# Hybrid encoder layer on one core: four modulation vectors in a lane of their own, last-norm rows on VectorE, causal mask on VectorE or GpSimd

## The chip, the cores and the metric

One core of one Trainium2 chip runs the whole layer in one launch. The metric is the device time of that launch in microseconds (us); a lower time is better. TensorE does the matrix products and the transposes, VectorE (DVE) and GpSimd (POOL) the elementwise work, ScalarE (ACT) the activations and some copies, and SyncE (SP) issues every DMA, in order.

## The reference, cut to what matters

```python
mod = (silu(c) @ w_ada + b_ada).reshape(bsz, 3, 3, 1024)      # nine vectors of 1024
f1 = _swiglu(_modulate(x, mod[:, 0, 0], mod[:, 0, 1]), ffn1_w_up, ffn1_w_down)
x = _post_norm(x, 0.5 * f1, mod[:, 0, 2], ln1_g, ln1_b)
tm = _token_mixer(_modulate(x, mod[:, 1, 0], mod[:, 1, 1]), w_in, ...)   # mLSTM heads | S5 groups
x = _post_norm(x, tm, mod[:, 1, 2], ln2_g, ln2_b)
f2 = _swiglu(_modulate(x, mod[:, 2, 0], mod[:, 2, 1]), ffn2_w_up, ffn2_w_down)
x = _post_norm(x, 0.5 * f2, mod[:, 2, 2], ln3_g, ln3_b)
```

There are 1024 tokens of 1024 channels, the hidden width of a feed-forward part is 2816, everything is float32. `_post_norm` is a layer norm of `alpha*x + (1+gate)*f`. The S5 part of the mixer needs tables (powers of a complex diagonal and products with its input and output matrices) that depend on parameters alone.

## The kernel before

**Products.** Each float32 operand is split into a high and a low part of a reduced type (`split`: a copy, then a subtraction), and a product is three matmuls 128x128 by 128x512 (`mm3`). All recorded times carry line 79, the place where the kernel's recording layer emits an instruction, so instructions are told apart by engine, shape and tile: `s` is any of 99 on-chip buffers of 256 KB, `b` a bank of PSUM.

**Feed-forward.** The first three column blocks of 128 of the hidden layer are plain products (`up_jobs`); the others come in pairs and are done by seven products in place of eight (`pair_jobs`, named by f = 3 and up; a pair job is 84 big matmuls). Their results go to DRAM as `Td`. The down projection does seven passes over the blocks (`product_jobs`, p = 5, 6, 3, 1, 7, 2, 4), which load `Td` and `in_w_down` (`w_down`) again. At the end of passes 1 and 7, sixteen and twelve VectorE instructions combine the four banks (`out`).

**Order.** TensorE's jobs run in a fixed list. All other work is written as generators in named lanes. A planner (`Clock`, `Kern.issue`) keeps a running clock of costs for every engine and, between TensorE's steps, takes from the lanes what is ready, earlier lanes first; each lane has a margin and a number of buffers that it must leave free (`LANES`). `nc.any` gives an addition or a product to VectorE or GpSimd, whichever the planner has free first. The program that results is fixed: every engine, and SP with it, runs its list in order.

**The lane `bg`** starts once the first modulated input is done. It computes the modulations 2 to 8 of the nine (`ada`; 0 and 1 are done in the start-up): for each, 16 loads of 256 KB of `in_w_ada`, 64 matmuls of 32 columns (`32x128` in the order, `128*32 128x128` in the trace, where each is recorded twice), and column sums with `one`. Then follow `affine` and `cols` for the later norms, and then `s5_gen`, which makes the S5 tables and stores them as `Wd`, `Vd`, `Md` and, last, sixteen `Ed`. The first norm waits for `("affine", 1)`, the S5 mixer for `("tables",)`.

**Last norm.** The last four hidden blocks are applied row tile by row tile (`end_jobs`): 8 transposes and 24 big matmuls for each of 8 tiles of 128 tokens. `end_ln` finishes a tile: copies and additions into buffers, statistics (`est`, `emv`), a reciprocal square root of some ten one-column instructions on `er` (`rsqrt`), then ScalarE scales and shifts, GpSimd (the first five tiles) or `any` multiplies by the gain and adds the bias. The last tile is done by two VectorE instructions per half instead.

**Mask.** In `mlstm`, sixteen additions on GpSimd (`P.tensor_tensor`) add the causal mask to blocks 128x512 before ScalarE's exponential.

Of the kernel before, what the change touches and what calls it, by code (L numbers as in the profile page):

```python
# [10 lines left out]
AF = mybir.ActivationFunctionType  # L11
OP = mybir.AluOpType
# [227 lines left out]
class Stream:  # L240
# [120 lines left out]
    def ensure(self, c):  # L361
        while self.ns <= min(c + AHEAD_SPLIT, len(self.chunks) - 1):
# [8 lines left out]
LANES = {"startl": (3.5, 20), "startx": (3.5, 2), "start": (3.5, 2), "startw": (3.5, 2), "startm": (4.5, 8),  # L371
# [3 lines left out]
WINDOW = 24  # L375
U, Q = ("u0", "u1", "u2", "u3"), ("q2", "q3", "q0", "q1")
IN_ORDER = ([(x, 0) for x in U + ("g", "q2")] + [(x, 1) for x in U + ("g", "q2")]
            + [(x, h) for x in Q[1:] + ("v", "o") for h in range(2)])
# [1 line left out]
S5_LATE = False  # L380
NACT = 4
SPARE = 8
END_POOL = 5
START_N = 1
START_A = 4
START_G = (0, 4), (4, 8)
# [9 lines left out]
class Kern:  # L396
# [483 lines left out]
    def pair_jobs(self, w_up, f, sub):  # L880
        nc, st = self.nc, self.st
        V = nc.vector
        cs = st.add_pair(*(w_up[f, u, :, 4 * y:4 * y + 4].rearrange("p k m -> p (k m)") for u in range(2) for y in range(2)))
        x = {}

        mix, block = {1: 0, 2: 1, 4: 2, 6: 3}, {0: (0, 0), 5: (4, 0), 3: (4, 1)}
        home, opens, closes = "adadaba", (0, 1, 5), (3, 5, 6)
        bank = {}  # L890

        def right(p, k):
            if p in mix:
                return self.T[mix[p]][k]
            k0, h = block[p]
            return self.Mh[k0 + k][h], self.Ml[k0 + k][h]

        def drop(p, k):
            if p in mix:
                self.T[mix[p]][k] = None  # L900
            else:
                k0, h = block[p]
                self.Mh[k0 + k][h] = self.Ml[k0 + k][h] = None

        def keep(n, b):
            x[n] = self.S()
            nc.scalar.activation(x[n], b, AF.Copy)

        def plus(n, b):
            V.tensor_tensor(x[n], x[n], b, op=OP.add)  # L910

        def out(p, b):
            if p in (0, 1, 2):
                keep(p, b)
            elif p == 3:
                plus(2, b)
                nc.scalar.activation(x[2], x[2], AF.Silu)
            elif p == 4:
                plus(1, b)
                nc.any.tensor_tensor(x[1], x[1], x.pop(2), op=OP.mult)  # L920
                self.hidden(sub, f, 1, x.pop(1))
            elif p == 5:
                plus(0, b)
                nc.scalar.activation(x[0], x[0], AF.Silu)
            else:
                g = x.pop(0)
                V.tensor_tensor(g, g, b, op=OP.mult)
                self.hidden(sub, f, 0, g)

        def job(p):  # L930
            def run():
                if f == NPLAIN[sub] and p == 0:
                    for k in range(4):
                        self.Mh[k][1] = self.Ml[k][1] = None
                if p in opens:
                    bank[home[p]] = self.bank()
                b = bank[home[p]]
                wh, wl = st.get(cs[p])
                for k in range(4):
                    c = slice(k * 128, (k + 1) * 128)  # L940
                    rh, rl = right(p, k)
                    mm3(nc, b, wh[:, c], wl[:, c], rh, rl, p in opens and k == 0, k == 3, p not in opens)
                    if f == NF - 1:
                        del rh, rl
                        drop(p, k)
                    if k == 1:
                        yield
                out(p, b)
                if p in closes:
                    self.free(b)  # L950
                yield
            return run

        for p in range(7):
            self.jobs.append(Job(cs[p], job(p), (("t", sub),) if f == NPLAIN[sub] and p == 0 else ()))
# [237 lines left out]
    def end_ln(self, t, banks):  # L1193
        nc = self.nc
        V = nc.vector
        st = self.small("est", [128, 2, 6], 4)
        mv = self.small("emv", [128, 2], 4)
        r = self.small("er", [128, 4], 4)
        xs = [self.S() for _ in range(2)]
        for y in range(2):  # L1200
            x = banks[y]
            if len(banks) == 4:
                nc.copy(xs[y], banks[2 + y])
                V.tensor_tensor(xs[y], xs[y], banks[y], op=OP.add)
                x = xs[y]
            V.bn_stats(st[:, y, :], x)
        V.bn_aggr(mv, st)
        V.tensor_scalar(r[:, 0:1], mv[:, 1:2], LN_EPS_S, None, op0=OP.add)
        last = len(banks) == 2
        for y in range(2 if last else 0):  # L1210
            V.scalar_tensor_tensor(xs[y], banks[y], mv[:, 0:1], self.gain[y], op0=OP.subtract, op1=OP.mult)
        self.rsqrt(r[:, 1:2], r[:, 0:1], r[:, 2:3])
        if not last:
            V.scalar_tensor_tensor(r[:, 3:4], mv[:, 0:1], -1.0, r[:, 1:2], op0=OP.mult, op1=OP.mult)
        for y in range(2):
            x = xs[y]
            if last:
                V.scalar_tensor_tensor(x, x, r[:, 1:2], self.gain[2 + y], op0=OP.mult, op1=OP.add)
            else:
                nc.scalar.activation(x, x, AF.Identity, scale=r[:, 1:2], bias=r[:, 3:4])  # L1220
                e = nc.gpsimd if t < END_POOL else nc.any
                e.tensor_tensor(x, x, self.gain[y], op=OP.mult)
                e.tensor_tensor(x, x, self.gain[2 + y], op=OP.add)
            nc.sync.dma_start(self.O["out"][t * 128:(t + 1) * 128, y * 512:y * 512 + 512], x)
        self.free(*banks)
        yield
# [918 lines left out]
    def mlstm(self):  # L2145
# [26 lines left out]
        for j, cs in enumerate(pairs):  # L2172
# [6 lines left out]
            for x, c in enumerate(cs):  # L2179
                hc, ts = self.tok(c)  # L2180
                mrs = ms[x]
                for d in range(2):
                    P.tensor_tensor(mrs[d], mrs[d], mk[:, d].unsqueeze(1).to_broadcast([128, 4, 128]), op=OP.add)
                sb = [self.bank(), self.bank()]
                for a in range(2):
                    nc.tensor.transpose(sb[0][:, (a + 2) * 128:(a + 3) * 128], qk[2 + a, hc][:, ts], self.ident)
                self.KT[c] = kt[:, x]
                nc.scalar.activation(self.KT[c], sb[0][:, 256:].rearrange("p (h x) -> p h x", h=4), AF.Copy)
                for a in range(2):
                    for p in range(2):  # L2190
                        l = slice(p * 64, p * 64 + 64)
                        nc.tensor.matmul(sb[p][:, a * 128:(a + 1) * 128], qk[2 + a, hc][l, ts], qk[a, hc][l, ts],
                                         start=True, stop=True)
                for d in range(2):
                    for h in range(4):
                        nc.scalar.activation(mrs[d][:, h, :], mrs[d][:, h, :], AF.Exp, scale=-1.0,
                                             bias=gc[:, c, 0, d, h:h + 1])
                    for p in range(2):
                        V.tensor_tensor(mrs[d][:, p::2, :], mrs[d][:, p::2, :],
                                        sb[p][:, :256].rearrange("p (h t) -> p h t", h=2), op=OP.mult)  # L2200
                    self.PT[d, c] = mrs[d]
                self.mark(("vis", c))
                del mrs
                ms[x] = None
                yield
# [129 lines left out]
    def run(self):  # L2335
# [6 lines left out]
        def background():  # L2342
            yield from self.wait(("m", 0, 1))
            yield from self.ada([2])
            self.cols(0, True)
            self.mark(("cols", 0))
            yield from self.ada(range(3, 9))
            self.cpad = None
            self.affine(1, "ln1_g", "ln1_b")
            self.cols(1, False)  # L2350
            self.affine(2, *(("ln2_g", "ln2_b") if mixer else ("ln1_g", "ln1_b")))
            self.cols(2, True)
            for x in (("affine", 1), ("affine", 2), ("cols", 1), ("cols", 2)):
                self.mark(x)
            if mixer:
                yield from self.s5_gen()
                self.mark(("tables",))

        self.later("bg", background())
        self.ffn(0, I["w_up1"], I["w_down1"], "ln1_g", "ln1_b", nxt, I["x"], skip=3,  # L2360
                 drains=((("m", 0, 0), ("pieces",)), (("m", 0, 1),)))
        if mixer:
# [87 lines left out]
```

## Time and profile before

| | us |
|---|---|
| median of 3 runs (lowest to highest) | 1933.21 (1928.89 to 1936.46) |
| the profiled execution, own time | 1935.63 |
| its span | 1933.8 |
| TensorE busy in the span | 1849.7 (96%), 10544 matmul records |
| VectorE busy | 1587.7 (82%) |
| ScalarE busy | 653.4 (34%) |
| GpSimd busy | 200.5 (10%) |

A busy time is the union of an engine's instructions; for TensorE their ends are modelled, so that a stretch with 100% can still hold fewer matmuls than fit. The chain that ended last is TensorE for 81% of the span, VectorE for 10% and DMA for 5%. The mean granted clock of TensorE is 0.981 of full speed.

### The profile page before, as it was taken

To read this page: it belongs to the slowest core of one execution; us is meant where nothing else is said; L and a number is where in the kernel's file an instruction comes from. 1 tells how busy PE (TensorE), PEld (TensorE's weight loads), DVE (VectorE), ACT (ScalarE), POOL (GpSimd) and SP (SyncE) were. 2 spreads that over 40 slices of the span, in tenths; PEclk is the share of its full clock that TensorE was granted. 3 is DMA by queue.
4 is the path that set the end of the run, shared out by engine and by line. 5 is a ranking of instruction groups with operands and counts; after the bars stand their busy time and mean duration, and the time that the engine had idled before them with its cause. 6 is when DMAs were issued, how large, how long until landed. Compare 5 with 4: busy or idle time off the path is not lost.

```text
span 1933.8 us, 29721 instructions
## 1 busy us (share of the span) xinstructions
PE 1849.7 (96%) x10544; PEld 1458.2 (75%) x10544; DVE 1587.7 (82%) x3296; ACT 653.4 (34%) x1204; POOL 200.5 (10%) x210
## 2 busy tenths in 40 slices
PE   6999999999999899999999998999999999999996
PEld 4667888777788677777787777678888888887775
DVE  7937889989899999868887796998677767597887
ACT  4512333333332325624444422542222222233412
POOL 0000000000000001100014401301111211000014
PEclk9999999999999989998999999999999999999998
DMA  9985233444493735572624544223232323574512
GB/s 324 317 300 192 82 113 115 158 132 141 149 341 117 259 132 190 161 259 100 207 72 150 177 149 157 77 102 111 88 122 96 105 82 109 181 255 143 183 44 76
DMA packets 188148, 303.13 MB, mean 157 GB/s; under 512 B 27792, under 2 KB 47440, under 8 KB 188000
## 3 DMA queue, kind: packets, MB, share of 16 engines
q1 hardware_dynamic: 188000, 301.24, 46.1%
q8 instruction: 83, 1.36, 0.3%
q14 instruction: 65, 0.53, 0.1%
HBM read 224.55 MB, written 76.61 MB: 156 GB/s over the span
## 4 chain that ended last, share of the span: by engine, by line
PE 81%; DVE 10%; DMA 5%; issue 2%; ACT 1%; SPq 1%; DVEq 0%; POOL 0%; ACTq 0%
PE b L79 81%; DVE s L79 8%; DMA s<-in_w_ada 2%; ACT s L79 1%; DMA s<-Vd 1%; SPq L79 1%; DMA s<-in_x 1%; DMA s<-in_w_down 1%; DVE er L79 0%; DMA s<-in_w_first 0%; DMA s<-in_w_f 0%; DMA s<-Td 0%; DVE mr L79 0%; DMA s<-in_w_out 0%; DVE st L79 0%
## 5 line engine op out<-in xcount | busy, mean ns | idle before, releaser
L79 PE MATMUL b<-s 128*128 128x512 f32 (+5 forms) x9208 | 1819.9, 372 | 50.8 <-DVE s L79 36.0
L79 PEld LDWEIGHTS b<-s 128*128 128x128 f32 (+3 forms) x9208 | 1417.0, 177 | 424.0 <-DVE s L79 51.8
L79 DVE TENSOR_TENSOR s<-s 128x512 fp32r<-128x512 f32 (+5 forms) x1767 | 997.6, 613 | 61.8 <-ACT s L79 28.3
L79 ACT ACTIVATE s<-s 128x512 fp32r<-128x512 f32 (+3 forms) x683 | 400.1, 624 | 591.6 <-DVE s L79 386.7
L79 DVE TENSOR_TENSOR s<-s,b 128x512 f32<-128x512 f32 (+1 forms) x340 | 214.8, 653 | 184.6 <-PE b L79 172.6
L79 POOL TENSOR_TENSOR s<-s 128x512 f32<-128x512 f32 (+1 forms) x117 | 169.4, 1464 | 1190.1 <-ACT s L79 502.1
L79 ACT ACTIVATE s<-b 128x512 f32<-128x512 f32 (+3 forms) x219 | 119.5, 553 | 458.8 <-PE b L79 425.0
L79 DVE CAST s<-s 128x512 fp32r<-128x512 f32 (+1 forms) x249 | 129.6, 524 | 7.7 <-DMA s<-in_x 2.7
L79 DVE SCALAR_TENSOR_TENSOR s<-b,gcol,s 128x512 f32<-128x512 f32 x56 | 39.5, 746 | 23.9 <-PE b L79 23.9
L79 ACT ACTIVATE s<-b,vec 128x128 f32<-128x128 f32 (+4 forms) x61 | 25.8, 485 | 88.6 <-PE b L79 82.4
L79 POOL MEMSET s<- 128x4 f32 (+6 forms) x62 | 6.9, 137 | 391.8 <-PE b L79 259.5
L79 PE MATMUL b<-ident,s 128*128 128x128 f32 (+1 forms) x208 | 30.9, 279 | 3.7 <-DVE s L79 3.7
L79 PEld LDWEIGHTS b<-ident,s 128*128 128x128 f32 (+1 forms) x208 | 25.2, 151 | 11.0 <-ACT s L79 4.3
L79 ACT ACTIVATE s<-s,vec 128x512 f32<-128x512 f32 x30 | 22.4, 782 | 19.4 <-DVE s L79 19.4
L79 DVE SCALAR_TENSOR_TENSOR s<-s 128x320 f32<-128x320 f32 (+3 forms) x43 | 22.8, 533 | 6.2 <-ACT s L79 6.0
L79 DVE TENSOR_TENSOR_SCAN s<-s 128x512 f32<-128x512 f32 (+2 forms) x22 | 24.1, 1121 | 4.4 <-POOL s L79 4.3
L79 DVE SCALAR_TENSOR_TENSOR s<-s,vec 128x512 f32<-128x512 f32 (+1 forms) x36 | 25.8, 737 | 0.1
L79 ACT ACTIVATE s<-s,Bp,Gp 128x512 f32<-128x512 f32 x23 | 17.7, 805 | 20.3 <-DVE s L79 20.3
L79 PEld LDWEIGHTS b<-one,s 128*32 128x32 f32 x576 | 8.5, 113 | 15.6 <-DVE s L79 12.2
L79 PE MATMUL b<-one,s 128*32 128x1 f32 x576 | 9.3, 174 | 11.4 <-DVE s L79 11.4
L79 DVE SCALAR_TENSOR_TENSOR s<-s,dec,b 128x129 f32<-128x129 f32 x24 | 8.1, 343 | 14.5 <-PE b L79 14.2
L79 ACT ACTIVATE s<-s,gcols 128x128 f32<-128x128 f32 x64 | 19.6, 394 | 0.2
(102 smaller groups left out, 328.4 us busy)
## 6 DMA issues: line engine op xcount, KB each, us to landing
s<-in_w_up SPq DMA_DIRECT2D x170, 256.0 KB
s<-in_w_ada SPq DMA_DIRECT2D x144, 256.0 KB
Td<-s SPq DMA_DIRECT2D x140, 256.0 KB
s<-Td SPq DMA_DIRECT2D x140, 256.0 KB
s<-in_w_down SPq DMA_DIRECT2D x124, 256.0 KB
Xd<-s SPq DMA_DIRECT2D x48, 256.0 KB
s<-Xd SPq DMA_DIRECT2D x48, 256.0 KB
s<-in_x SPq DMA_DIRECT2D x32, 256.0 KB
```

The costliest lines, as they stand in the source:

```text
L79: self.eng, self.alts, self.emit = eng, (), lambda: getattr(real, name)(*args, **kw)
```

## The change

Lane `bg` now does modulations 2, 3 and 4, then `affine(1)`, then the S5 tables at once. Modulations 5 to 8 with `cols(1)`, `affine(2)` and `cols(2)` move to a new lane `bg2`, last in priority, which waits for the flag `("pair", 0, 5)` that the first job of pair f = 5 of the first feed-forward sets. `end_ln` does every tile as the last one was done: two `scalar_tensor_tensor` on VectorE per half, none of it on ScalarE or GpSimd. The mask addition is given to `any`.

```diff
-         "lv": (3.0, 10), ..., "conv": (2.5, 6), "bg": (3.5, 6)}
+         "lv": (3.0, 10), ..., "conv": (2.5, 6), "bg": (3.5, 6), "bg2": (3.5, 8)}
+LATE = ("pair", 0, 5)
...
+                if p == 0:
+                    self.flags.add(("pair", sub, f))
...
-        last = len(banks) == 2
-        for y in range(2 if last else 0):
-            V.scalar_tensor_tensor(xs[y], banks[y], mv[:, 0:1], self.gain[y], op0=OP.subtract, op1=OP.mult)
+        for y in range(2):
+            x = xs[y] if len(banks) == 4 else banks[y]
+            V.scalar_tensor_tensor(xs[y], x, mv[:, 0:1], self.gain[y], op0=OP.subtract, op1=OP.mult)
         self.rsqrt(r[:, 1:2], r[:, 0:1], r[:, 2:3])
-        if not last:
-            V.scalar_tensor_tensor(r[:, 3:4], mv[:, 0:1], -1.0, r[:, 1:2], op0=OP.mult, op1=OP.mult)
         for y in range(2):
             x = xs[y]
-            if last:
-                V.scalar_tensor_tensor(x, x, r[:, 1:2], self.gain[2 + y], op0=OP.mult, op1=OP.add)
-            else:
-                nc.scalar.activation(x, x, AF.Identity, scale=r[:, 1:2], bias=r[:, 3:4])
-                e = nc.gpsimd if t < END_POOL else nc.any
-                e.tensor_tensor(x, x, self.gain[y], op=OP.mult)
-                e.tensor_tensor(x, x, self.gain[2 + y], op=OP.add)
+            V.scalar_tensor_tensor(x, x, r[:, 1:2], self.gain[2 + y], op0=OP.mult, op1=OP.add)
...
-                    P.tensor_tensor(mrs[d], mrs[d], mk[:, d]..., op=OP.add)
+                    nc.any.tensor_tensor(mrs[d], mrs[d], mk[:, d]..., op=OP.add)
...
-            yield from self.ada(range(3, 9))
+            yield from self.ada([3, 4])
+            self.affine(1, "ln1_g", "ln1_b")
+            self.mark(("affine", 1))
+            if mixer:
+                yield from self.s5_gen()
+                self.mark(("tables",))
+
+        def rest():
+            yield from self.wait(LATE)
+            yield from self.ada(range(5, 9))
             self.cpad = None
-            self.affine(1, "ln1_g", "ln1_b")
             self.cols(1, False)
             ...
-            if mixer:
-                yield from self.s5_gen()
-                self.mark(("tables",))
         self.later("bg", background())
+        self.later("bg2", rest())
```

The planner orders everything anew. Three places follow, as the built programs have them.

SP's list of DMAs in the first feed-forward's down projection, kernel before, from the middle of pass p = 1 (`Ed` are stores of S5 tables, `in_x` loads of the residual, of which each of the passes 3, 1, 7 and 2 has one group of four):

```order
L79 DMA s<-in_x 128x512 x4
L79 DMA Ed<-s 128x512
L79 DMA s<-Td_91 128x512
L79 DMA s<-Td_92 128x512
L79 DMA Ed<-s 128x512
L79 DMA s<-in_w_down 128x512
L79 DMA s<-Td_93 128x512
L79 DMA Ed<-s 128x512 x2
```

The same place in the changed program:

```order
L79 DMA s<-in_x 128x512 x4
L79 DMA s<-Td_91 128x512
L79 DMA s<-Td_92 128x512
L79 DMA s<-in_w_down 128x512
L79 DMA s<-Td_93 128x512
L79 DMA s<-in_w_down 128x512
L79 DMA s<-Td_94 128x512
L79 DMA s<-in_w_down 128x512
```

Before, all sixteen `Ed` stores stand behind the first group of `in_x` loads, that of pass 3; now fourteen stand ahead of it and two right behind it, and none behind the second group.

TensorE's list of the changed program where modulation 4 ends and modulation 5 begins (`32x128` are modulations, `32x1` their column sums, `128x512` big matmuls):

```order
L79 MATMUL b<-s 128x512 x6
L79 MATMUL b<-one,s 32x1 x16
L79 MATMUL b<-s 128x512 x282
L79 MATMUL b<-s 32x128 x12
L79 MATMUL b<-s 128x512 x6
L79 MATMUL b<-s 32x128 x12
```

Before, groups of modulations and groups of six big matmuls alternate without such a gap until the last modulation is done; now 282 big matmuls stand between the third and the fourth of the seven. Counted over TensorE's first 1950 big matmuls, a group of others follows a group of big ones 88 times before and 94 times now.

VectorE's list in the last norm, one of the middle tiles, kernel before (`emv` are a tile's mean and variance, `er` the columns of its reciprocal root):

```order
L79 TENSOR_TENSOR s<-s,b 128x512 x2
L79 BN_STATS est<-s 128x6
L79 SCALAR_TENSOR_TENSOR er<-er 128x1
L79 BN_STATS est<-s 128x6
L79 SCALAR_TENSOR_TENSOR er<-er 128x1
L79 BN_AGGR emv<-est 128x2
L79 TENSOR_SCALAR er<-emv 128x1
L79 TENSOR_TENSOR er<-er 128x1
```

And in the changed program:

```order
L79 TENSOR_TENSOR s<-s,b 128x512 x2
L79 BN_STATS est<-s 128x6
L79 SCALAR_TENSOR_TENSOR er<-er 128x1
L79 BN_STATS est<-s 128x6
L79 TENSOR_TENSOR er<-er 128x1
L79 BN_AGGR emv<-est 128x2
L79 SCALAR_TENSOR_TENSOR er<-er 128x1
L79 TENSOR_SCALAR er<-emv 128x1
L79 SCALAR_TENSOR_TENSOR s<-s,emv 128x512 x2
```

A tile's two centring instructions (`s<-s,emv`) now stand behind its variance, and two scaling ones (`s<-s,er`) follow its reciprocal root. Twenty-eight such instructions of 128x512, in all, are new on VectorE there; twenty products and additions leave GpSimd and eight leave VectorE, and fourteen activations leave ScalarE. Of the sixteen mask additions nine go to VectorE, the first four among them, and seven stay on GpSimd.

## Rows read from the trace of the kernel before

**Rows 1.** Stretches: length, busy us (instructions) by engine, granted clock, DMA share, GB/s

```profile
52.00:162.00 110.00, 108.59 (x1638) 76.30 (x1628) 68.62 (x135) 38.59 (x75) 7.64 (x4) 1.00 0.89 310
162.00:654.00 492.00, 492.00 (x2367) 392.38 (x2357) 449.11 (x1037) 162.83 (x289) 6.39 (x19) 1.00 0.45 152
654.00:760.00 106.00, 93.04 (x439) 73.55 (x438) 104.23 (x175) 32.83 (x56) 7.20 (x5) 0.92 0.57 198
...
1775.00:1816.00 41.00, 36.20 (x149) 28.58 (x148) 37.68 (x61) 17.25 (x30) 0.00 (x0) 0.96 0.51 164
...
1300.00:1350.00 50.00, 50.00 (x218) 40.46 (x217) 43.04 (x70) 11.25 (x19) 6.86 (x5) 1.00 0.38 132
...
550.00:650.00 100.00, 100.00 (x433) 81.01 (x432) 94.88 (x172) 32.90 (x58) 3.46 (x2) 1.00 0.62 218
```

**Rows 2.** TensorE's groups by form in 654 to 760: count, busy, mean ns, idle

```profile
L79 PE MATMUL b<-s 128*128 128x512 f32 x369 | 92.3, 411 | 12.2 <-DVE s L79 12.2
```

**Rows 3.** The chain that ended last, 650 to 762: start, us, what

```profile
666.39 4.98 DMA s<-in_w_down
671.38 4.58 DMA s<-Td
...
704.46 4.00 DMA s<-in_w_down
708.53 5.26 DMA s<-in_x
```

**Rows 4.** SP's queue in time, 640 to 760: start, us, what was issued

```profile
684.23 0.32 SPq L79 DMA_DIRECT2D s<-Td  x1
698.90 0.32 SPq L79 DMA_DIRECT2D Ed<-s  x1
...
708.53 2.28 SPq L79 DMA_DIRECT2D s<-in_x  x4
723.53 3.34 SPq L79 DMA_DIRECT2D Ed<-s  x2
```

**Rows 5.** TensorE's groups by form in 52 to 162, the stretch of modulations

```profile
L79 PE MATMUL b<-s 128*128 128x512 f32 x279 | 76.0, 410 | 0.0
L79 PE MATMUL b<-s 128*32 128x128 f32 x896 | 34.7, 278 | 1.4 <-DMA s<-in_w_ada 1.2
```

**Rows 6.** Groups by form in 1860 to 1934, the last norm

```profile
L79 POOL TENSOR_TENSOR s<-s 128x512 f32<-128x512 f32 x20 | 25.2, 1289 | 63.6 <-ACT s L79 63.5
L79 DVE SCALAR_TENSOR_TENSOR er<-er 128x1 f32<-128x1 f32 x48 | 12.1, 261 | 0.5
...
L79 DVE TENSOR_TENSOR er<-er 128x1 f32<-128x1 f32 x24 | 8.5, 353 | 0.3
```

**Rows 7.** VectorE in time, last norm: start, us for all, what, count

```profile
1871.86 1.28 DVE L79 TENSOR_TENSOR s<-s,b 128x512 f32<-128x512 f32 x2
1873.05 1.28 DVE L79 BATCH_NORM_STATS2 est<-s 128x6 f32<-128x512 f32 x2
...
1876.74 0.16 DVE L79 SCALAR_TENSOR_TENSOR er<-emv,er 128x1 f32<-128x1 f32 x1
...
1907.16 0.15 DVE L79 TENSOR_TENSOR er<-er 128x1 f32<-128x1 f32 x1
...
1917.88 1.18 DVE L79 TENSOR_TENSOR er<-er 128x1 f32<-128x1 f32 x1
...
1929.47 1.41 DVE L79 SCALAR_TENSOR_TENSOR s<-s,er 128x512 f32<-128x512 f32 x2
```

**Rows 8.** GpSimd and TensorE in time, last norm

```profile
1911.56 8.83 POOL L79 TENSOR_TENSOR s<-s 128x512 f32<-128x512 f32 x7 [2.41 <-ACT s L79]
...
1912.00 5.79 PE L79 MATMUL b<-s 128*128 128x512 f32 x24
```

**Rows 9.** Groups by form in 1028 to 1145, the mLSTM stretch

```profile
L79 POOL TENSOR_TENSOR s<-s 128x512 f32<-128x512 f32 x18 | 24.5, 1394 | 2.4 <-DMA s<-Wr 2.4
...
L79 DVE TENSOR_TENSOR s<-s 128x512 f32<-128x512 f32 x6 | 4.5, 771 | 0.0
```

More of the change, by code (lines that the diff above doesn't have):

```diff
@@ L382 @@
 SPARE = 8
-END_POOL = 5
 START_N = 1
@@ L2182, in mlstm @@
                 for d in range(2):
-                    P.tensor_tensor(mrs[d], mrs[d], mk[:, d].unsqueeze(1).to_broadcast([128, 4, 128]), op=OP.add)
+                    nc.any.tensor_tensor(mrs[d], mrs[d], mk[:, d].unsqueeze(1).to_broadcast([128, 4, 128]), op=OP.add)
                 sb = [self.bank(), self.bank()]
@@ L2352, in background @@
             self.cols(2, True)
-            for x in (("affine", 1), ("affine", 2), ("cols", 1), ("cols", 2)):
+            for x in (("affine", 2), ("cols", 1), ("cols", 2)):
                 self.mark(x)
-            if mixer:
-                yield from self.s5_gen()
-                self.mark(("tables",))
         self.later("bg", background())
+        self.later("bg2", rest())
         self.ffn(0, I["w_up1"], I["w_down1"], "ln1_g", "ln1_b", nxt, I["x"], skip=3,
```

2 rows, old and new, of the table LANES are left out of this document.

## The prediction

> **What bounds the kernel now.** I read the view of stretches first: TensorE's busy time and VectorE's beside it, stage by stage [rows 1]. Where TensorE runs at its own pace it does 218 big matmuls in 50 us, 0.230 us each (1300 to 1350). From 162 to 654, the pair products, it is busy all of 492 us, with VectorE at 449.1 of 492 (91%); from 550 to 650 VectorE stands at 94.9 of 100 and TensorE still loses nothing. From 654 to 760, the end of the first down projection, VectorE is full, 104.2 of 106 us, and TensorE's clock falls to 0.92: it did 369 big matmuls there [rows 2], 369 x 0.230 = 84.9 us, and some 70 small ones, 2.4 us by the price below, so 106 - 84.9 - 2.4 = 18.7 us are lost. The second feed-forward's down projection has the same passes without the S5 tables; it loses, from 1775 to 1816, 41 - 149 x 0.230 = 6.7 us.
>
> The chain of waits says how the loss comes about [rows 3]: twice TensorE waits for weights that were asked for late, at 666 and at 704. SP's queue in time gives the reason [rows 4]: after a load at 684.2 it issues nothing for 14 us, until an `Ed` store, whose data VectorE has not yet made, goes out at 698.9; the loads queued behind it follow at once. It stands still again until 723.5. So in this stretch the tables cost twice, as VectorE work and as stores that hold back an in-order queue.
>
> At the other end, TensorE's last big matmuls end at 1912.0 + 5.8 = 1917.8 [rows 8] and VectorE's last instruction at 1929.5 + 1.4 = 1930.9 [rows 7]; the span ends 2.9 us later. The last norm is VectorE's.
>
> **Tables out of the down projection.** By SP's list fourteen of the sixteen `Ed` stores now stand ahead of the first residual loads, none behind the second. Each stands for three VectorE instructions of 128x512 at 1.28 / 2 = 0.64 us [rows 7]; nine were stored after 653.8, three of them in [rows 4], so about 9 x 3 x 0.64 = 17 us of 104 leave, and VectorE is at 87 of 106, no longer the bound. What is late next is the combining work at the ends of passes 1 and 7, which the second feed-forward shows at 6.7 us. Gain 18.7 - 6.7 = 12.0; I take **-11**, since the next norm's first work starts in the same stretch. Bounds: 0, if other work fills the room, to -18.7.
>
> **Where the tables go.** 16 x 3 x 0.64 = 31 us of VectorE work enter the pair products, and four modulations give that stage 26 us more of TensorE (below): (449 + 31) / (492 + 26) = 93%, under the 95% at which TensorE lost nothing [rows 1]. That hides it; I take **+1**. If the cover is gone, it is the slow rival.
>
> **Four modulations moved.** From 52 to 162 the seven modulations cost TensorE 110 - 279 x 0.230 = 45.8 us beside the big matmuls [rows 5] (the other 1638 - 279 = 1359 records [rows 1] then cost 0.034 us each, waits for loads in it). Four of seven are 26.2 us, paid now, by TensorE's list, among 168 big matmuls of the pairs: the same work elsewhere. Two things can differ. By the lists groups of other matmuls follow big ones 94 times for 88, some 30 of these in the old stretch; a group costs at most 45.8 / 30 = 1.5 us, its work included; for the switch alone I take a fifth of it, 0.33, and 6 x 0.33 = **+2** (bounds 0 to +9). And the loads: 64 of `in_w_ada`, 8 of `w_up` and 8 stores stand between them on SP, 80 x 0.262 MB = 21 MB in 168 x 0.230 + 26.2 = 64.8 us, 324 GB/s, where the old stretch moved 310 GB/s with its 16 DMA engines 89% busy [rows 1]. At 310 they need 67.7 us, and weights queued behind them come up to 3 us late; against that, the waits for `in_w_ada` in the old stretch (1.2 us seen) shrink: **+0.7** (bounds -2 to +5). TensorE's share between, 282 big matmuls without a modulation, waits for nothing that is new.
>
> **Last norm on VectorE.** Before a tile: two additions 1.28, two statistics 1.28, a run of small instructions from 1874.3 to 1876.9, 2.6 us [rows 7]. Added: four `scalar_tensor_tensor` at 1.41 / 2 = 0.70, 2.8 us. Alone that is 8.0 a tile; but the order puts the small ones of one tile between the large ones of the next, and half of their 2.6 hidden gives 6.7. I take 7.0, against TensorE's 6.4 (24 big matmuls, 5.8, and the transposes). From 1871.9: seven tiles to 1920.9, the eighth 1.28 + 2.57 + 2.8 to 1927.5, the store 2.9: 1930.4 for 1933.8, **-3.4**. The 8 products that leave VectorE and the wait for ScalarE and GpSimd at the end are what pays for it. Bounds: 6.7 gives -5.5.
>
> The upper bound comes from the small instructions. While GpSimd worked, from 1911.6 on [rows 8], one of one column took 1.18 us; with GpSimd idle, at 1907.2, 0.15 [rows 7]. The change leaves GpSimd idle there. At the means with GpSimd at work, 0.261 and 0.353 [rows 6], they make 3.1 us a tile, which is the second rival's price.
>
> The Trainium skill ("SBUF — State Buffer", section "Who interferes with whom") has it that a VectorE instruction with two inputs in SBUF and a GpSimd instruction that reads SBUF exclude each other for the whole instruction. The trace agrees: 1.18 us is about one GpSimd product (8.83 / 7 = 1.26). By that rule the small ones cost 0.15 once GpSimd is out; without it, the second rival.
>
> **Mask.** Nine of sixteen additions move from GpSimd, at 1.39, to VectorE, at 0.77 [rows 9]: 7 us more on VectorE across four pairs of chunks, while the first blocks come sooner. Queued behind them on VectorE are the products with the scores. **-0.5** (bounds -3 to +4).
>
> **Sum.** -11 + 1 + 2 + 0.7 - 3.4 - 0.5 = -11.2. Against the profiled execution's own 1935.6: 1924.4. That execution lies 2.4 above the median of its runs, so for the median **1922.0**, own range 1914 to 1930.
>
> **Rivals.** First, the down projection keeps its loss: passes' ends and the next norm fill VectorE again, and the term is 0, not -11: 1933. For it speaks that much of VectorE's work there is not the tables'; against it that the second feed-forward runs the same passes at 6.7.
>
> Second, VectorE becomes the bound of the last norm at the means of [rows 6]: 1.28 + 1.28 + 3.1 + 2.99 = 8.7 a tile; 7 x 8.7 + 8 from 1871.9 is 1940.8, with the store 1943.7, +10 for -3.4: 1935. Against it: those means hold waits for GpSimd. The Trainium skill ("Perfetto Trace Analysis", section "Optimizing Scalar/DVE Operations") advises to offload from a saturated VectorE, even to GpSimd, and in the same breath warns that the two share a port. Its first half is this rival; no run shown here decides it.
>
> Third, slower: VectorE runs full in the pair products, where the tables and the moved modulations meet, for the 160 us or so from pair 5 on. The price is that of the one stretch in which it was full, 18.7 / 106 = 0.18 us lost per us, 28 us: 1922 - 1 + 28 = 1949. It decides from between 95% (nothing lost) and 98% (104.2 of 106). For it: 31 us in a stage at 91%; against it the 26 us that the stage grows by. That the change does not do what it says, tables no earlier, is out by SP's list.
>
> **How the numbers follow.** About 0.5%, 9.7 us, is what a measurement of this kernel can tell from no change. Forecast 0.63 (0.53 under 1923.5, 0.10 above); first rival 0.12, no change; second 0.14, 0.13 of it no change; third 0.11, slower. Faster 0.53, same 0.35, slower 0.12. The range 1911 to 1940 takes in the forecast's bounds and both middle rivals and leaves out the third.
>
> **What would show it.** Right: in the down projection's stretch VectorE under 95%, no SP pause ahead of an `Ed`, the granted clock above 0.92; TensorE busy all through the pairs; in the last norm no one-column instruction of 1 us, the end 12 to 14 us after the last big matmul. Wrong: TensorE's waits on `DVE s` between pairs, VectorE without a pause there, or a last norm in which tiles follow each other by 8 us and more.

## The result, and the profile after

The changed kernel took a median of 1910.7 us in 6 runs (1908.4 to 1919.2), the kernel before beside it 1933.7; the ratio is 0.9888, with a 95% interval from 0.9862 to 0.9914. A second set of runs of the same kernel, further below, gave 1908.6 us and 0.9867 (0.9841 to 0.9893). So it is faster, by 22 to 26 us. The direction is the one forecast. The time lies at the very edge of the range 1911 to 1940 (the second set a little under it) and outside the forecast's own 1914 to 1930, and the gain is about twice the 11.2 us that were summed. The profiled execution took 1908.43 us, its span 1906.6, with a mean granted clock of 0.987 where before had 0.981.

The page of the changed kernel, busy time by engine and the shares of the chain that ended last:

```profile
PE 1841.5 (97%) x10544; PEld 1453.0 (76%) x10544; DVE 1588.2 (83%) x3306; ACT 646.8 (34%) x1201; POOL 166.5 (9%) x182
...
PE 84%; DVE 10%; DMA 3%; issue 2%; ACT 1%; SPq 0%; POOL 0%; DVEq 0%; POOLq 0%
```

TensorE has 84% of the chain, for 81 before, and DMA 3 for 5; VectorE's busy time is the same 1588 us in a span 27 us shorter. The stretches of the changed kernel that answer to [rows 1]: length, busy us and instructions of PE, PEld, DVE, ACT, POOL, then granted clock, DMA share, GB/s:

```profile
52.00:162.00 110.00, 109.45 (x967) 83.03 (x966) 98.79 (x265) 42.06 (x75) 3.24 (x1) 1.00 0.54 189
162.00:654.00 492.00, 491.62 (x3005) 385.34 (x3004) 439.17 (x944) 162.85 (x293) 7.91 (x21) 1.00 0.55 191
...
654.00:760.00 106.00, 99.38 (x469) 78.76 (x468) 94.85 (x160) 40.08 (x69) 7.23 (x4) 0.95 0.45 146
```

From 52 to 162 TensorE has 967 records in place of 1638: four of the seven modulations have left. In the pairs it is busy all the time still, with VectorE at 439 of 492. From 654 to 760 VectorE is at 94.9 of 106 (89%) and TensorE at 99.4, for 104.2 and 93.0 before.

Every trace has the same 6944 records of matmuls of 512 columns, so that the n-th of them is the same work in all kernels. The table gives the time between such marks, in us: up to the 186th (start-up; from the next one on TensorE's lists differ), to the 2316th (modulations, pairs, first three passes), to the 2844th (the passes 1, 7, 2, 4), to the S5 mixer's first matmul (rest of the first norm and of the in-projection), to the run of 144 big matmuls that ends the mixer, to the second norm's first matmul with `meanw` (the mLSTM and the output projection), to the first of the last 24, and to the end of the span. "Before's lists" are the profiles of this kernel and of the runs below that keep its lists in that stretch, "new lists" those with the change's; with the count of profiles.

| stretch | before | changed | before's lists | new lists |
|---|---|---|---|---|
| to 186 | 97.2 | 96.7 | the same lists in both: 96.4 to 100.4 | |
| to 2316 | 543.7 | 542.8 | 542.3 to 543.9 (5), mean 543.5 | 542.8 to 543.2 (7), mean 542.9 |
| to 2844 | 142.8 | 136.3 | 142.7 to 142.9 (4), mean 142.8 | 134.7 to 136.3 (7), mean 135.4 |
| to S5 | 44.5 | 40.5 | 44.3 to 44.8 (5), mean 44.6 | 39.9 to 40.5 (7), mean 40.1 |
| S5 mixer | 124.5 | 117.1 | 117.4 to 124.5 (5) | 116.3 to 122.5 (8) |
| to second norm | 255.9 | 252.0 | 255.9 to 260.7 (8), mean 257.6 | 251.4 to 252.0 (3), mean 251.8 |
| to the last 24 | 703.5 | 704.4 | 703.5 to 704.2 (6) | 703.6 to 706.4 (7), mean 704.3 |
| to the end | 21.8 | 17.0 | 21.8 to 21.9 (6) | 17.0 to 17.1 (6), 18.2 (1) |

### The profile page after: what moved, and what is told of

Read it like the earlier page. It is cut to its first block, busy times and chain, and to the rows that moved or that the text cites. A ratio compares the mean times of both kernels' runs of the same rounds, so it can differ in the third digit from the quotient of the medians.

```text
span 1906.6 us, 29677 instructions
## 1 busy us (share of the span) xinstructions
PE 1841.5 (97%) x10544; PEld 1453.0 (76%) x10544; DVE 1588.2 (83%) x3306; ACT 646.8 (34%) x1201; POOL 166.5 (9%) x182
## 4 chain that ended last, share of the span: by engine, by line
PE 84%; DVE 10%; DMA 3%; issue 2%; ACT 1%; SPq 0%; POOL 0%; DVEq 0%; POOLq 0%
PE b L79 84%; DVE s L79 9%; DMA s<-in_w_ada 1%; DMA s<-Vd 1%; ACT s L79 1%; DMA s<-in_x 0%; SPq L79 0%; POOL s L79 0%; DMA s<-in_w_first 0%; DVE lnv L79 0%; DMA s<-Td 0%; DMA Ud<-s 0%; DMA s<-Ud 0%; DVE gv L79 0%; DVE er L79 0%
## 5 line engine op out<-in xcount | busy, mean ns | idle before, releaser
L79 PE MATMUL b<-s 128*128 128x512 f32 (+6 forms) x9208 | 1813.4, 371 | 39.0 <-DVE s L79 26.9
L79 PEld LDWEIGHTS b<-s 128*128 128x128 f32 (+4 forms) x9208 | 1412.2, 176 | 409.5 <-DVE s L79 45.5
L79 ACT ACTIVATE s<-s 128x512 fp32r<-128x512 f32 (+4 forms) x680 | 399.0, 625 | 557.7 <-DVE s L79 409.2
L79 ACT ACTIVATE s<-b 128x512 f32<-128x512 f32 (+2 forms) x220 | 119.7, 553 | 461.2 <-PE b L79 410.6
L79 POOL TENSOR_TENSOR s<-s 128x512 f32<-128x512 f32 (+2 forms) x88 | 132.8, 1520 | 1158.4 <-ACT s L79 566.8
L79 DVE CAST s<-s 128x512 fp32r<-128x512 f32 x252 | 128.1, 511 | 8.5 <-DMA s<-in_x 3.2
L79 DVE SCALAR_TENSOR_TENSOR s<-s,vec 128x512 f32<-128x512 f32 (+1 forms) x36 | 25.7, 734 | 0.1
L79 PE MATMUL b<-one,s 128*32 128x1 f32 x576 | 9.4, 174 | 11.9 <-DVE s L79 11.9
L79 DVE SCALAR_TENSOR_TENSOR s<-s,gcol 128x512 f32<-128x512 f32 x24 | 18.3, 764 | 0.6
```

The lines of the kernel that those rows point to most:

```text
L79: self.eng, self.alts, self.emit = eng, (), lambda: getattr(real, name)(*args, **kw)
```

## The experiments

**The three parts alone, and two of them.** The lists of the engines show that the parts don't touch each other: the lanes' end in the S5 mixer, the mask begins in the mLSTM, the norm's edit changes only the last norm. So each was built alone on the kernel before, and lanes and norm together. The lanes (`background` and `rest` as in the change, norm and mask as before):

> The lanes alone: tables ahead of the four modulations, norm and mask as before. Theory 1 (all of the gain up to the last norm comes from the lanes, that in the first norm, the in-projection and the S5 mixer too, since TensorE's, VectorE's and SP's lists differ from those of before only up to there): 1933 - 9.5 (down projection) - 10.7 (norm, in-projection and S5 mixer) - 1.4 (all ahead of them) + 3 (the next norm's first part) = about 1915, ratio 0.990. Theory 2 (what the S5 mixer gained is only how that one profiled execution fell out): the down projection's -8.3 alone, 1925, ratio 0.9957, and the S5 mixer, measured between the same two instructions, as long as before.

Measured 0.9924 (0.9904 to 0.9945), a median of 1919.1: 14.7 us of 1933.6, between the two theories. In its trace the first norm starts 9.1 us sooner than before, the S5 mixer 11.1 and its end 18.8; after that nothing is gained. Of the 18.8, 7.6 are the S5 mixer's, which a later paragraph takes up. The norm alone:

> The last norm alone: the lists of all engines are those of before up to the last 24 big matmuls' stretch. Theory: the tail after the last big matmul falls from 16.0 to 11.5 us, and nothing else moves: 1933 - 4.5 = 1928.5, ratio 0.9977. Rival (VectorE becomes the bound, tiles follow each other by more than TensorE's 6.4 us): the last big matmul itself ends 3 us and more later and the gain is under 1.5 us, ratio above 0.999. Its profile is also a second look at the first 1860 us of the kernel before.

Measured 0.9975 (0.9959 to 0.9992), 4.8 us. The tail from the start of the last 24 big matmuls is 17.1 us for 21.8, and what lies ahead of it took 703.6 for 703.5. The rival is out: VectorE does not slow TensorE there. The mask alone:

```diff
-                    P.tensor_tensor(mrs[d], mrs[d], mk[:, d]..., op=OP.add)
+                    nc.any.tensor_tensor(mrs[d], mrs[d], mk[:, d]..., op=OP.add)
```

> The mask alone: the lists are those of before up to the mLSTM stretch. Theory 1 (the 4 us that the changed kernel is ahead of before at the end of the mLSTM stretch are the mask's): 1933 - 4 = 1929, ratio 0.998. Theory 2 (they are a matter of how the execution fell out, or of the lanes): 1933 - 0.5, ratio 0.9997. Its profile is also a third look at the first 1028 us of the kernel before: if the slow clock stretch at 890 us and the S5 mixer's length are the same there, they belong to the kernel and not to the execution.

Measured 0.9986 (0.9967 to 1.0005), which by itself decides nothing. Its stretch to the second norm took 251.4 us, under every profile without the mask's edit (255.9 and more). Lanes and norm without it:

> The changed kernel less its mask: lanes and norm together, the sixteen mask additions on GpSimd as before. Theory 1 (the parts add): 0.9924 x 0.9975 = 0.990, 4 to 5 us above the changed kernel, the whole difference between the S5 mixer's last matmul and the second norm (257 us for 252) and nothing at the tail, 17.0 us from the last 24 big matmuls' start. Theory 2 (the mask's gain is only how executions fell out, its own run gave 0.9986 with 1 inside the interval): ratio 0.988 and the stretch at 252. It is also one more look at the clock in the S5 mixer with the lanes' lists.

Measured 0.9904 (0.9885 to 0.9922), and 257.7 us in that stretch: theory 1 by the trace; the intervals of the ratio with and without the mask overlap. The three single ratios multiply to 0.9885, the change measured 0.9888 and 0.9867. The parts add.

**What the tables cost in the down projection.** The prediction named two costs: VectorE's work, and stores that hold SP's loads back [rows 4]. The first run takes only the stores away. The sixteen `Ed` stores of the kernel before are issued by GpSimd; the lists of TensorE, VectorE and ScalarE stay word for word:

```diff
-                nc.sync.dma_start(self.Ed[b, c], t1...)
+                nc.add(Op("d", nc.gpsimd.real, "dma_start", (self.Ed[b, c], t1...), {}))
```

> The kernel before, with the sixteen Ed stores issued by GpSimd in place of SP: the lists of TensorE, VectorE and ScalarE stay word for word, SP loses the sixteen stores. Theory 1 (the down projection's loss is SP's: loads of weights and of the residual held behind stores whose data is late): the waits of TensorE for in_w_down and Td at 666 and 704 go, 654 to 760 gets 6 to 9 us shorter, 1925, ratio 0.996. Theory 2 (the loss is VectorE's, full by 31 us of table work in the stretch): the loads come early and the same data is late on VectorE instead, 0 to 2 us, ratio 0.999 to 1.000.

Measured 1.0002 (0.9988 to 1.0015): theory 2. SP's queue in time of this run shows that the hold is gone: the residual that was asked for at 708.5 before [rows 4] goes out at 703.3, the next loads right behind it (start, us, what):

```profile
703.28 1.80 SPq L79 DMA_DIRECT2D s<-in_x  x4
705.18 0.86 SPq L79 DMA_DIRECT2D s<-Td  x2
```

What was late is now VectorE's work. The chain that ended last, 650 to 762, kernel before and this run:

```profile
by line: PE b L79 66.5%; DMA s<-in_w_down 13.0%; DMA s<-in_x 4.7%; DMA s<-in_w_f 4.1%; DMA s<-Td 4.1%; DVE s L79 3.1%; issue 2.2%; SPq L79 1.4%; ACT s L79 1.2%; DVE lnv L79 0.1%
by line: PE b L79 53.7%; DVE s L79 39.4%; issue 4.7%; DMA s<-in_w_down 2.2%; DVEq L79 0.2%
```

TensorE waits as long as before. Its waits in 654 to 760, kernel before (us, times, longest; PEld are the weight loads):

```profile
PEld b L79 <- DVE s L79: 13.5, 3, 8.1
...
PE b L79 <- DVE s L79: 12.2, 2, 7.7
```

of this run:

```profile
PEld b L79 <- DVE s L79: 14.6, 4, 9.2
...
PE b L79 <- DVE s L79: 12.9, 3, 8.7
```

and of the changed kernel:

```profile
PEld b L79 <- DVE s L79: 8.3, 4, 3.9
PE b L79 <- DVE s L79: 6.6, 3, 3.5
```

So the late loads of [rows 3] were late ahead of an engine that had no time for them. The second run puts the work back and no store: lanes as in the change, and 27 sums, differences and copies of 128x512 on VectorE issued twice from the end of the third pass on. Some of the doubled sums are done in place and so are added twice: the output of this kernel is not the layer's.

```diff
         op.emit()
+        if self.K.twice and op.eng == "v" and op.wide and not op.w & op.r:
+            self.seen += 1
+            if self.seen % 2 == 0:
+                self.K.twice -= 1
+                op.emit()
```

> The lanes as in the run of the lanes alone, and 27 VectorE instructions of 128x512 (sums, differences and copies whose result does not change when they are done again) issued twice from the middle of the down projection's third pass on: 27 x 0.66 = 18 us of VectorE work, about what the nine late table groups were, with no store and no change in any other engine's list. Theory 1 (the loss of the down projection is VectorE's work): VectorE has some 8 to 10 us of room ahead of the end of pass 1, so 8 to 10 us come back, 1919 + 9 = 1928, ratio 0.997, and TensorE's waits on VectorE in the stretch are again above 20 us. Theory 2 (the loss was something else that came with the tables, such as their stores, buffers or TensorE's transposes): as the lanes alone, 1919, ratio 0.9924.

Measured 0.9964 (0.9951 to 0.9977), 1929.7 us: 0.0040 above the lanes alone, 7.7 us come back for 18 us of work: theory 1. The passes took 141.2 us, for 134.9 with the lanes alone and 142.8 before, and TensorE's waits for VectorE in 654 to 760 are 10.3 us (weight loads 13.0), for 7.0 and 8.7 with the lanes alone. Where the room was shows in one stretch of the lanes alone and of this run, 654 to 662 (columns as above):

```profile
654.00:662.00 8.00, 8.00 (x36) 6.51 (x35) 0.00 (x0) 1.20 (x3) 0.00 (x0) 1.00 0.72 233
```

That is the lanes alone, and this the run with work put back:

```profile
654.00:662.00 8.00, 8.00 (x36) 6.50 (x35) 7.43 (x13) 1.26 (x2) 0.00 (x0) 1.00 0.58 193
```

With the tables gone VectorE does nothing for 8 us ahead of the end of pass 1, and TensorE works on. The third run makes the tables early without a second lane and its flag; the modulations 5 to 8 follow them in `bg`:

```diff
-            yield from self.wait(LATE)
             yield from self.ada(range(5, 9))
...
                 self.mark(("tables",))
+            yield from rest()
```

> The tables ahead of the four modulations, but in one lane and with no flag, norm and mask as before: the planner then makes the sixteen table groups between the 1812th and the 2334th big matmul (with the lane of their own between the 1650th and the 2289th, before between the 2283rd and the 2708th), since VectorE has less room in the pairs, and the modulations follow in the down projection. Theory 1 (only where VectorE's table work lies counts): nothing of it is left at the ends of passes 1 and 7, so nearly all of the lanes' gain, 1933 - 11 = 1922, ratio 0.994. Theory 2 (the four modulations in the pairs are what gives VectorE its room, and in the down projection their loads and column sums cost what the tables did): within 4 us of before, ratio 0.998 or more.

Measured 0.9941 (0.9920 to 0.9962), 1924.8 us: most of the lanes' gain, and theory 1. From the 186th to the 2844th big matmul it takes 679.3 us, the lanes alone 677.9, before 686.5. What counts is that the table work is off the ends of the passes; the second lane adds a little, and the two intervals overlap.

**The last norm.** The norm alone, and for each tile four GpSimd products of 128x512 whose results nobody reads, so that GpSimd is busy there again (40.7 us in all, 25.2 before):

```diff
+        g, m = self.gain[0].ap, mv[:, 0:1].to_broadcast([128, 512])
+        def idle():
+            for _ in range(4):
+                w = self.sb.tile([128, 512], F32, ...)
+                nc.gpsimd.real.tensor_tensor(w, g, m, op=OP.mult)
+        nc.fill.append(idle)
```

> The last norm alone as in the run of the norm alone, and four products of 128x512 on GpSimd for each tile, from its variance on, whose results nobody reads: 4 x 1.26 = 5 us of GpSimd work in a tile's 6.4, with the other engines' lists unchanged. Theory 1 (part of the gain is that VectorE's one-column instructions no longer wait for GpSimd): they are back at means of 0.26 to 0.35 us in place of 0.15, 13 x 0.15 = 2 us a tile, VectorE falls behind TensorE and the tail after the last big matmul grows from 11.5 to 15 us or more: 1929 + 4 = 1933, ratio 0.9995. Theory 2 (the gain is the shorter chain alone): tail and time as with the norm alone, ratio 0.9975.

Measured 1.0059 (1.0042 to 1.0076), 1946.9 us: by the ratios 16 us above the norm alone, four times what theory 1 said. VectorE's list is that of the norm alone; its groups by form in the last norm of the changed kernel (count, busy us, mean ns, idle ahead):

```profile
L79 DVE SCALAR_TENSOR_TENSOR s<-s,er 128x512 f32<-128x512 f32 x16 | 11.2, 747 | 0.1
L79 DVE SCALAR_TENSOR_TENSOR s<-s,emv 128x512 f32<-128x512 f32 x14 | 9.9, 743 | 0.0
L79 DVE TENSOR_TENSOR s<-s,b 128x512 f32<-128x512 f32 x14 | 9.4, 685 | 1.5 <-PE b L79 1.5
...
L79 DVE SCALAR_TENSOR_TENSOR er<-er 128x1 f32<-128x1 f32 x48 | 6.7, 152 | 0.7
```

and with GpSimd busy:

```profile
L1213 POOL TENSOR_TENSOR s<-s,emv 128x512 f32<-128x512 f32 x32 | 40.7, 1302 | 67.0 <-issue 45.7 <-DVE emv L79 12.2 <-PE b L79 5.4
...
L79 DVE SCALAR_TENSOR_TENSOR s<-s,emv 128x512 f32<-128x512 f32 x14 | 16.2, 1189 | 0.0
L79 DVE SCALAR_TENSOR_TENSOR er<-er 128x1 f32<-128x1 f32 x48 | 15.3, 330 | 0.7
L79 DVE SCALAR_TENSOR_TENSOR s<-s,er 128x512 f32<-128x512 f32 x16 | 14.4, 945 | 0.1
...
L79 DVE TENSOR_TENSOR s<-s,b 128x512 f32<-128x512 f32 x14 | 9.1, 678 | 0.0
```

The one-column instructions are back at 330 ns (261 in [rows 6]), but the large ones with two operands from SBUF grow as well, 743 to 1189 and 747 to 945 ns: 6.2 + 8.5 + 3.2 = 18 us. My expectation had only the small ones. The addition with one operand from PSUM (`s<-s,b`) stays where it was. GpSimd and VectorE in time, one tile of this run:

```profile
1893.95 5.05 POOL L1213 TENSOR_TENSOR s<-s,emv 128x512 f32<-128x512 f32 x4 [3.46 <-DVE er L79]
```

The second engine, VectorE, in the same time:

```profile
1896.02 0.14 DVE L79 TENSOR_SCALAR er<-er 128x1 int32<-128x1 int32 x1
1896.09 0.93 DVE L79 SCALAR_TENSOR_TENSOR er<-er 128x1 f32<-128x1 f32 x1
1896.93 0.15 DVE L79 TENSOR_TENSOR er<-er 128x1 f32<-128x1 f32 x1
1897.11 0.90 DVE L79 SCALAR_TENSOR_TENSOR er<-er 128x1 f32<-128x1 f32 x1
1897.93 1.61 DVE L79 SCALAR_TENSOR_TENSOR s<-s,er 128x512 f32<-128x512 f32 x1
1899.46 0.14 DVE L79 SCALAR_TENSOR_TENSOR er<-er 128x1 f32<-128x1 f32 x1
```

While the four products run, to 1899.0, two one-column `SCALAR_TENSOR_TENSOR` take 0.93 and 0.90 us, and the one right after takes 0.14. The `TENSOR_TENSOR` between them takes 0.15: not every one waits, and why this one doesn't, the trace does not show.

**The mask.** The changed kernel with all sixteen additions on VectorE, and with eight on each engine, by direction:

```diff
-                    nc.any.tensor_tensor(mrs[d], mrs[d], mk[:, d]..., op=OP.add)
+                    V.tensor_tensor(mrs[d], mrs[d], mk[:, d]..., op=OP.add)
```

> The changed kernel with all sixteen mask additions on VectorE in place of nine: GpSimd is out of the mLSTM's chain altogether. Theory 1 (the mask's gain is the first blocks' earlier start, which nine on VectorE give already): the same as the changed kernel within 2 us, 1911, ratio 0.988. Theory 2 (the gain is that GpSimd's 1.39 us additions go): 7 more of them gone, 2 to 3 us more, 1908, ratio 0.987. Theory 3 (VectorE is full in that stretch): 7 x 0.66 = 4.6 us slower, 1915, ratio 0.990. Its list is the changed kernel's up to the mLSTM stretch: another look at whether the clock stays full in the S5 mixer.

```diff
-                    nc.any.tensor_tensor(mrs[d], mrs[d], mk[:, d]..., op=OP.add)
+                    (V if d == 0 else P).tensor_tensor(mrs[d], mrs[d], mk[:, d]..., op=OP.add)
```

> The changed kernel with the sixteen mask additions dealt out by hand, the eight of one direction to VectorE and the eight of the other to GpSimd, in place of nine and seven as the planner's free engine has it. Theory 1 (the mask's gain is that about half of the additions leave GpSimd, so that the two engines work on a block pair side by side): as the changed kernel, 1911, ratio 0.988 to 0.989, from the mLSTM's first product to the second norm 160 to 162 us. Theory 2 (the gain hangs on the order that the planner made of it, one of many): the stretch is as long as with GpSimd alone or VectorE alone, 164 to 167 us, 1915, ratio 0.990 to 0.991.

All on VectorE measured 0.9906 (0.9884 to 0.9927), near theory 3's figure, its stretch 258.8 us, as long as with all on GpSimd. Eight and eight measured 0.9886 (0.9861 to 0.9910), an interval that takes in both theories; by its stretch, 253.4 us, it is theory 1. TensorE's waits for VectorE from the end of the S5 mixer to the second norm, kernel before and changed kernel:

```profile
PE b L79 <- DVE s L79: 7.5, 4, 3.7
PE b L79 <- DVE s L79: 3.2, 3, 2.1
```

and with all on VectorE, and with eight and eight:

```profile
PE b L79 <- DVE s L79: 8.0, 6, 3.7
PE b L79 <- DVE s L79: 3.2, 5, 1.6
```

In all, TensorE is idle in that stretch for 10.2, 5.8, 10.7 and 6.5 us, in the same order; what is left of the differences in length goes with the granted clock, 0.98 in the first two and 0.97 in the last two. So the wait more than halves when the additions are shared, and not when either engine has them all.

But the planner moved more than the additions. VectorE's instructions of 128x128 in the same stretch, kernel before:

```profile
L79 DVE TENSOR_SCALAR s<-s,mr 128x128 f32<-128x128 f32 x25 | 7.9, 341 | 0.1
L79 DVE TENSOR_SCALAR s<-b,dn 128x128 f32<-128x128 f32 x20 | 5.6, 345 | 0.2
```

changed kernel, where the thirteen that are missing are on ScalarE:

```profile
L79 DVE TENSOR_SCALAR s<-b,dn 128x128 f32<-128x128 f32 x16 | 4.8, 344 | 0.1
L79 DVE TENSOR_SCALAR s<-s,mr 128x128 f32<-128x128 f32 x16 | 4.8, 341 | 0.1
```

and all on VectorE:

```profile
L79 DVE TENSOR_SCALAR s<-s,mr 128x128 f32<-128x128 f32 x25 | 7.9, 339 | 0.1
L79 DVE TENSOR_SCALAR s<-b,dn 128x128 f32<-128x128 f32 x23 | 6.7, 344 | 0.3
```

With eight and eight eleven of them go to ScalarE. So VectorE is no busier in the changed kernel than before, 201 us of the stretch, and 196 with eight and eight; with all on VectorE it has 208. That the gain comes with the edit is shown. Whether it is the shared additions or the work that VectorE gave to ScalarE in the same two builds, no run separates.

**The S5 mixer.** No term of the prediction stands for the 7.4 us by which it got shorter. In both kernels TensorE waits there for ScalarE, 3.07 us before and 3.08 after. Behind that wait the granted clock is half (1.2 for 2.4 GHz) for 10 us in the trace of before, and full in that of the changed kernel. The same 20 us, kernel before:

```profile
889.00:909.00 20.00, 19.99 (x122) 15.26 (x122) 16.59 (x27) 12.93 (x33) 0.82 (x5) 0.74 0.38 129
```

with the stores on GpSimd, all of TensorE's work there in before's order:

```profile
889.00:909.00 20.00, 20.00 (x143) 15.58 (x143) 19.65 (x32) 13.04 (x34) 0.92 (x6) 1.00 0.47 160
```

and lanes and norm without the mask, all of it in the change's order:

```profile
875.00:895.00 20.00, 19.16 (x103) 14.54 (x104) 15.64 (x25) 13.51 (x36) 0.62 (x6) 0.67 0.34 107
```

The clock stands at 1.00 with before's lists and at 0.67 with the new ones, so the lists don't decide it. Inside the mixer, moreover, TensorE, VectorE, ScalarE and GpSimd do the same work in the same order in all thirteen profiles counted below, by operation, shape and tile. The changed kernel once more:

> The changed kernel itself once more. Theory 1 (its S5 mixer is shorter than before's by 7 us because of the change): 117 us between the mixer's first matmul and its last big ones, clock full, as in its first profile; ratio 0.9888. Theory 2 (the half clock there comes and goes between executions): 117 or 122 to 124 us as it falls out, and a median of the two sets of runs between 0.988 and 0.990.

Measured 0.9867; 117.6 us in the mixer, clock full. Over all profiles the mixer takes 116.3 to 117.8 us where the clock stays full (6, one of them with before's lists), and 121.7 to 124.5 where it falls (7). It fell in 4 of 5 with before's lists and in 3 of 8 with the new ones. Whether the change makes it rarer stays open; that it shortens the mixer otherwise is out. One run tried to take the wait away: the copies of the gate rows that ScalarE does ahead of the two evictions go to GpSimd.

```diff
+                if f == AF.Copy:
+                    nc.gpsimd.tensor_copy(y[h][F], x[h][F])
+                    nc.gpsimd.tensor_copy(y[h][B], x[1 - h][B, ::-1])
+                    continue
```

> The changed kernel with eight copies of the mLSTM's gate rows (32 and 4 partitions by 512, six of them in ScalarE's 3.5 us run at 870) given to GpSimd in place of ScalarE. In the S5 mixer TensorE waits 3.1 us for two evictions queued behind that run on ScalarE, and in most profiles the clock then falls to half for 10 us. Theory 1 (the wait goes, and the half clock with it): 3 us with a full clock, up to 8 us where it had fallen, 1907 to 1908, ratio 0.986. Theory 2 (the evictions then stand behind something else, or the new order costs elsewhere what is gained): 1911 or more, ratio 0.988 or more.

Measured 0.9884 (0.9861 to 0.9908), no better than the change. TensorE's waits in its mixer:

```profile
PE b L79 <- DMA s<-Vd: 3.7, 4, 2.1
PE b L79 <- ACT s L79: 2.1, 3, 0.9
```

No wait of 3 us is left, but the `Vd` loads are now waited for, 3.7 us in all, and the clock falls all the same (0.83 from 880 to 900): theory 2. No run beat the changed kernel.

## Why the prediction was right, and where its sizes were off

**Tables out of the down projection, -11.** The passes gave 7.4 us (142.8 to 135.4), 3.6 less than the term. The rest of the first norm and of the in-projection gave 4.5 more (44.6 to 40.1), for which the sum has no term: its words on the next norm's first work take 1 us off the gain. That the two make 11.9, near 11, is in part luck. Of the mechanism half holds: VectorE's work in the passes was the cost, as putting work back showed. "In this stretch the tables cost twice", the second time as stores in an in-order queue, is wrong: without the stores nothing was gained. The chain of [rows 3] names the transfer that came last, not the engine that had no time for it sooner; [rows 2] had named VectorE already. VectorE, forecast at 87 of 106 us, came out at 94.9, and "VectorE under 95%, clock above 0.92" at 89% and 0.95, but the SP pause ahead of an `Ed` was no sign of anything. Part of the 7.4 is the clock: TensorE idles 12.6 to 13.3 us in the passes with before's lists and 6.6 to 7.2 with the new ones, and its granted clock is half for 17.1 us there before and for 3.4 to 10.2 with the new lists. Where the 4.5 come from stays open: with the work put back into the passes that stretch still took 40.1 us. What the traces show there is some ten VectorE instructions fewer (54 for 65), and TensorE's 2.5 us of waits for VectorE gone.

**What the moves cost, +1, +2 and +0.7.** Together nothing that can be told: 543.5 before, 542.9 with the new lists, for the 3.7 that I summed. The pairs hide the table work and the moved loads; the third rival, VectorE full there at +28, did not come near: TensorE is busy 491.6 of 492. The first, the loss kept, is out by the 7.4. Which of the three terms was too large no run separates.

**Last norm, -3.4.** It gave 4.8 (21.8 to 17.0). The tile's pace is the mis-sized step: I took 7.0 us, so that VectorE would be 3 us behind at the last matmul. The order packs a tile closer than that. TensorE's last matmuls in time, changed kernel:

```profile
1889.56 5.80 PE L79 MATMUL b<-s 128*128 128x512 f32 x24
```

and VectorE's last tile, from its statistics to its end:

```profile
1894.70 0.70 DVE L79 BATCH_NORM_STATS2 est<-b 128x6 f32<-128x512 f32 x1 [0.97 <-PE b L79]
...
1902.27 1.41 DVE L79 SCALAR_TENSOR_TENSOR s<-s,er 128x512 f32<-128x512 f32 x2
```

VectorE waits 0.97 us for TensorE ahead of the last tile; it is not behind. From the last matmul's end at 1895.4 to VectorE's end at 1903.7 are 8.3 us, where before had 1930.9 - 1917.8 = 13.1; the end of the span comes 11.2 us after the last matmul, for "12 to 14". The second rival rested on the means of [rows 6]; they are 152 ns now, for 261 and 353, and no one-column instruction takes 1 us (the longest 0.16).

The Trainium skill ("SBUF — State Buffer", section "Who interferes with whom") had it that a VectorE instruction with two inputs in SBUF and a GpSimd one that reads SBUF exclude each other. The run with GpSimd busy agrees, 152 to 330 ns and 743 to 1189, and the addition with an operand from PSUM, which by that page does not contend, stayed at 678.

**Mask, -0.5.** It gave 5.8 us in the traces (257.6 to 251.8), 3 to 7 in the ratios (0.9904 to 0.9888 and 0.9867). This step failed in size and in reason. "The first blocks come sooner" would hold with all additions on VectorE as well, and there nothing was gained; "7 us more on VectorE" did not come, since the planner took as much from it; my bounds, -3 to +4, did not reach it. I had priced the additions by their own durations and never asked how long TensorE is idle in that stretch, 10.2 us before, 7.5 of them for VectorE; that would have shown what there was to gain.

**The sum.** -0.6 - 7.4 - 4.5 - 5.8 - 4.8 = -23.1, and the ratios say -21.6 and -25.7. The profiled pair differs by 27.2: 20.1 in these stretches, 7.4 in the S5 mixer with its clock, 0.5 in the start-up, less 0.9 in the second feed-forward. So the direction was right for the reason given in two of the four parts (tables, norm). The moves were too dear by 4.3, the mask was missed by 5.3, the norm by 1.4, and 4.5 had no term of their own. All of these err to the same side.

## What to carry to other kernels

An in-order queue that stands still ahead of late data is a symptom as long as the engine behind it is full: first ask which engine makes the data late, and take its work away, or test it by issuing the stores elsewhere. Work that depends on nothing belongs where the bounding engine has room, and the ends of accumulation passes, where one engine's burst lets another wait, are where it has none. Where GpSimd shares a stretch with VectorE, count all of VectorE's instructions with two operands in SBUF as dearer, the large ones too. Before pricing a small edit in a stretch, read how long the bounding engine waits there; and where a planner orders the program, count afterwards what else it moved.

## What the runs showed of the hardware

TensorE's granted clock fell to half during or right after the same wait of 3.1 us in 7 of 13 profiles and stayed full in the others, with the same lists on both sides; the mixer was 4 to 7 us longer each time than the 117 us it takes otherwise. In the twelve timed runs of the changed kernel the time goes with the mean granted clock: 0.986 to 0.990 in the eight up to 1910.8 us, 0.983 to 0.985 in the four above. A gain that shows behind such a wait in one pair of profiles needs a third.

The Trainium skill ("TensorE: Matmul & The Clock Gate", section "Part 1: The HAM clock gate (the "warmup" mystery)") says that the gate runs on its own time, not from the kernel's start, and that one kernel therefore meets it differently from run to run. The traces agree that executions differ: 0.74, 1.00 and 0.67 behind the same wait, above. That the gate's own time is the reason, no run here shows.

Four GpSimd products a tile, 5 us in 6.4, cost VectorE 18 us over eight tiles, and the kernel 16, though GpSimd's own products took 1302 ns, hardly more than those of [rows 6] (1289): the price fell on VectorE.
